# Differential attention on one core: a head's two token tiles taken together, with scores by eight products on all 128 rows

## The chip, the cores and the metric

The kernel runs on one core of a Trainium2 chip. The metric is the device time of one execution in microseconds (us). A core has a matrix engine (TensorE, in the profile PE, with its weight loads as PEld), two engines for element-wise work (VectorE, DVE, and ScalarE, ACT), GpSimd (POOL) and a DMA queue on SyncE (SP). PE multiplies a stationary operand (its weights, at most 128 rows by 128 columns) with a moving one and adds the result into PSUM, a small memory of eight banks of 512 float32 columns. All else lies in SBUF, on 128 partitions ("rows" below). PE executes its instructions strictly in the order of the program text.

## The reference

Two decoder layers on 256 tokens of width 2048, all in float32. Each layer does this, cut to what matters here:

```
h   = RMSNorm(x);  P = h @ W_in          columns [q | k | v | gate_B | gate_C | conv_in], 1024 each
q,k = RMSNorm over 64 numbers            8 heads x 2 maps x 64
s   = q_m k_m^T / 8 + bias, causal       m = 0, 1: two score maps per head
A   = (softmax(s_0) - lam softmax(s_1)) @ v, RMSNorm per head, times a gain
Cv  = gate_B * conv3(gate_C * conv_in)
x   = x + concat([A, Cv]) @ W_out
x   = x + relu(RMSNorm(x) @ W_up)^2 @ W_down
```

A head has 128 columns of q and k, 64 for each map, and 128 of v. The tokens are two tiles of 128. By causality the first tile sees 128 keys, the second 256.

## The kernel before, in words

**Arithmetic.** Every float32 operand is split into a high part (rounded for PE) and a low part (the rest). A product is three products: high x high, high x low, low x high (`TERMS`, line 38). Weights are split as they arrive: `Weights.halves` (line 277) writes `whi` on ScalarE (line 285) and `wlo` on VectorE (line 286).

**Order of PE's work.** The text gives it, and it is manual for PE. In `mixer` (line 602) two halves of four heads each compute q, k and v with `linear` (line 328: a 512-column product for each tile, term and 128 input columns), then follow four gc/ci pairs and four gb products with `linear_t` (line 347: eight products of 512 columns and eight of 256 for each group of weights) and the output projection. Three groups of weights are made ahead (`AHEAD`).

**Ticks.** Small pieces are put between these products. A piece is a Python generator in `Background` (line 55); it yields the number of ticks until it goes on. `linear` ticks after every six products, `linear_t` after every four. So the first half's attention runs among the second half's q, k and v products, and the second half's among the first gc and ci products. `staggered` (line 85) starts the units of an attention some ticks apart.

**q and k.** `qk_norm` (line 458) normalizes a half's q or k, waits 8 ticks, transposes each token tile on PE (line 481) and writes high and low parts with one ScalarE copy (line 484) and one VectorE operation (line 485). Each head's 128 rows hold map 0 in rows 0 to 63 and map 1 in rows 64 to 127.

**Attention.** `attention` (line 489) has a unit for each of 2 tiles x 4 heads, 4 ticks apart, all first tiles ahead of all second tiles:

- scores `sc` (line 503): for each map three products on that map's 64 rows, of 128 or 256 columns;
- bias and row maximum on VectorE (line 506), negation (511), exponentials with their sums on ScalarE (513), reciprocal, c and p on VectorE (516 to 524); 9 ticks after the scores the transposes of p, `ptp` (529), and its split `pT` (531, 532);
- 4 ticks later the products with v, `av` (539): three for each 128 keys, of 128 columns, into one bank for four heads. After the fourth head the bank is copied out (547), squared and normalized (552 to 559), and 9 ticks later transposed (`atp`, 565) and written in parts to `cat` (568, 569), an input of the output projection.

PSUM has three rotating banks for `sc`, `ptp` and the other transposes, one for `av`, and two pairs for the long products. The engines other than PE get their order from the framework's scheduler, and run it in order.

**Setup.** Gains, the bias table and lambda vectors are loaded on POOL's queue at the start (lines 168 to 183) into buffers of their own and used by `small_setup` (line 199) and `load_bias` (line 230).

Of the kernel before, what the change touches and what calls it, by code (L numbers as in the profile page):

```python
# [9 lines left out]
F32 = mybir.dt.float32  # L10
# [91 lines left out]
def trunk(ctx: ExitStack, tc: tile.TileContext, x, w_in, w_out, conv_w, q_norm_g, k_norm_g,  # L102
# [8 lines left out]
    nat = ctx.enter_context(tc.tile_pool(name="nat", bufs=7))  # L111
# [19 lines left out]
    const.tile([P, 40], F32, tag="fill", name="fill")  # L131
# [36 lines left out]
    vec = const.tile([ROWS, P], F32, tag="vec", name="vec")  # L168
    nc.gpsimd.dma_start(vec[0:NCW, :], conv_w.rearrange("l i (k p) -> (l i k) p", p=P))
    for i, g in enumerate((q_norm_g, k_norm_g)):  # L170
        for m in range(2):
            nc.gpsimd.dma_start(
                vec[QG + i * DEPTH:QG + (i + 1) * DEPTH, m * DK:(m + 1) * DK], g)
    nc.gpsimd.dma_start(vec[QG + 2 * DEPTH:MG, :], subln_g)
    nc.gpsimd.dma_start(vec[MG:ROWS, :], mlp_norm_g.rearrange("l (k p) -> (l k) p", p=P))
    lamv = const.tile([1, 4, DEPTH, DK], F32, tag="lamv", name="lamv")
    for i, a in enumerate((lambda_q1, lambda_q2, lambda_k1, lambda_k2)):
        nc.gpsimd.dma_start(lamv[:, i], a[None])
    sel = const.tile([NB + 1, REL], F32, tag="sel", name="sel")
    nc.gpsimd.dma_start(sel, selector)  # L180
    rel = const.tile([NB + 1, 2 * NH], F32, tag="rel", name="rel")
    nc.vector.memset(rel[NB:NB + 1, :], NEG)
    nc.gpsimd.dma_start(rel[0:NB, :], rel_bias)
# [15 lines left out]
    def small_setup():  # L199
# [3 lines left out]
        by_dist = const.tile([2 * NH, REL], F32, tag="bydist", name="by_dist")  # L203
# [12 lines left out]
        prod = const.tile([1, 2, DEPTH, DK], F32, tag="lprod", name="lprod")  # L216
# [13 lines left out]
    def load_bias(l, bpool, bias):  # L230

        if l == 0:
            yield from small_setup()
        revs = []
        for j in range(2):
            rev = bpool.tile([P, NH, S], F32, tag="b", name=f"rev{l}{j}")
            src = by_dist_d[j * NH:(j + 1) * NH, 0:S]
            nc.gpsimd.dma_start(
                rev, bass.AP(src.tensor, src.offset, [[1, P], [REL, NH], [1, S]]))
            revs.append(rev)  # L240
        yield 4
        for h in range(0, NH, 2):
            for j in range(2):
                late(nc.scalar.activation(bias[:, j * NH + h:j * NH + h + 2],
                                          revs[j][:, h:h + 2, ::-1], AF.Copy))
            yield 2
# [141 lines left out]
    class Norm:  # L388
# [31 lines left out]
        def factors(self):  # L420
            while not all(t.ready for t in self.tiles):
                yield 1
            tot = small.tile([P, NT], F32, tag="tot", name="tot")
# [5 lines left out]
            if self.which:  # L429

                self.scale = small.tile([P, 1], F32, tag="rowf2", name="rowf2")
                nc.vector.tensor_mul(self.scale, r[:, 1:2], r[:, 1:2])
                ratio = small.tile([P, 1], F32, tag="ratio", name="ratio")
# [24 lines left out]
    def qk_norm(acc, r, dst, gain, name):  # L458
# [18 lines left out]
        yield 8  # L477
        for t in range(NT):
            tp = bank(f"{name}tp{t}")
            for i in range(4):  # L480
                nc.tensor.transpose(tp[:, i * P:(i + 1) * P], out_[t][:, i * P:(i + 1) * P], ident)
            tp3 = tp.rearrange("p (h c) -> p h c", c=P)
            hi, lo = (dst[:, i, :, t * P:(t + 1) * P] for i in range(2))
            nc.scalar.activation(hi, tp3, AF.Copy, scale=gain)
            nc.vector.scalar_tensor_tensor(lo, tp3, gain, hi.bitcast(F32),
                                           op0=ALU.mult, op1=ALU.subtract)
            yield 1

    def attention(l, qT, kT, v, h0, dst, bias, tmp):

        parts = dst.open()
        avs, r0s = {}, {}

        def unit(t, i):
            W = (t + 1) * P
            h = h0 + i
            s = tmp.tile([P, 2, S], F32, tag="s", name=f"s{h}_{t}")
            mx = small.tile([P, 2], F32, tag="mx", name=f"mx{h}_{t}")
            su = small.tile([P, 2], F32, tag="su", name=f"su{h}_{t}")
            for m in range(2):  # L500
                sc = bank(f"sc{h}_{t}_{m}")
                for n, (a, b) in enumerate(TERMS):
                    nc.tensor.matmul(  # L503
                        sc[:, :W], qT[m * DK:(m + 1) * DK, a, i, t * P:(t + 1) * P],
                        kT[m * DK:(m + 1) * DK, b, i, :W], start=(n == 0), stop=(n == 2))
                nc.vector.tensor_tensor_reduce(
                    out=s[:, m, :W], in0=sc[:, :W], in1=bias[:, 2 * h + m, S - W:],
                    op0=ALU.add, op1=ALU.max, scale=1.0, scalar=-3.0e38,
                    accum_out=mx[:, m:m + 1])
            nm = small.tile([P, 2], F32, tag="nm", name=f"nm{h}_{t}")  # L510
            nc.vector.tensor_scalar_mul(nm, mx, -1.0)
            for m in range(2):
                nc.scalar.activation(s[:, m, :W], s[:, m, :W], AF.Exp, bias=nm[:, m:m + 1],
                                     accum_out=su[:, m:m + 1])
            rc = small.tile([P, 2], F32, tag="rc", name=f"rc{h}_{t}")
            nc.vector.reciprocal(rc, su)
            if i == 0:
                r0s[t] = small.tile([P, 4], F32, tag="r0", name=f"r0_{h0}_{t}")
            nc.vector.tensor_copy(r0s[t][:, i:i + 1], rc[:, 0:1])
            c = small.tile([P, 1], F32, tag="c", name=f"c{h}_{t}")  # L520
            nc.vector.scalar_tensor_tensor(c, su[:, 0:1], rc[:, 1:2], nlam[:, l:l + 1],
                                           op0=ALU.mult, op1=ALU.mult)
            p = tmp.tile([P, S], F32, tag="p", name=f"p{h}_{t}", bufs=2)
            nc.vector.scalar_tensor_tensor(p[:, :W], s[:, 1, :W], c, s[:, 0, :W],
                                           op0=ALU.mult, op1=ALU.add)
            yield 9
            tp = bank(f"ptp{h}_{t}")
            for b in range(t + 1):
                nc.tensor.transpose(tp[:, b * P:(b + 1) * P], p[:, b * P:(b + 1) * P], ident)
            pT = tmp.tile([P, 2, S], F32R, tag="pT", name=f"pT{h}_{t}", bufs=2)  # L530
            nc.scalar.activation(pT[:, 0, :W], tp[:, :W], AF.Copy)
            nc.vector.tensor_sub(pT[:, 1, :W], tp[:, :W], pT[:, 0, :W].bitcast(F32))
            yield 4
            if i == 0:
                avs[t] = ps.tile([P, CH], F32, tag="av", name=f"av{h0}_{t}", bufs=1)
            av = avs[t]
            for k in range(t + 1):
                for n, (a, b) in enumerate(TERMS):
                    nc.tensor.matmul(  # L539
                        av[:, i * P:(i + 1) * P], pT[:, a, k * P:(k + 1) * P],  # L540
                        v[:, b, k, i * P:(i + 1) * P],
                        start=(k == 0 and n == 0), stop=(k == t and n == 2))
            if i < 3:
                return
            r0 = r0s[t]
            ao = wide(f"ao{h0}_{t}")
            nc.scalar.activation(ao, av, AF.Copy)
            ss = small.tile([P, 4], F32, tag="ams", name=f"ams{h0}_{t}")
            junk = wide(f"asq{h0}_{t}")
            for b in range(4):  # L550
                c = slice(b * P, (b + 1) * P)
                nc.scalar.activation(junk[:, c], ao[:, c], AF.Square, accum_out=ss[:, b:b + 1])
            for _ in range(2):
                nc.gpsimd.tensor_tensor(ss, ss, r0, op=ALU.mult)
            f = rstd_of(ss, P, f"a{h0}_{t}", 4)
            f2 = small.tile([P, 4], F32, tag="af2", name=f"af2{h0}_{t}")
            nc.gpsimd.tensor_tensor(f2, f, r0, op=ALU.mult)
            an = wide(f"an{h0}_{t}")
            nc.vector.tensor_tensor(
                an.rearrange("p (g d) -> p g d", d=P), ao.rearrange("p (g d) -> p g d", d=P),  # L560
                f2.unsqueeze(2).to_broadcast([P, 4, P]), op=ALU.mult)
            yield 9
            tp = bank(f"atp{h0}_{t}")
            for b in range(4):
                nc.tensor.transpose(tp[:, b * P:(b + 1) * P], an[:, b * P:(b + 1) * P], ident)
            tp3 = tp.rearrange("p (h c) -> p h c", c=P)
            hi = parts[:, 0, :, t * P:(t + 1) * P]
            nc.scalar.activation(hi, tp3, AF.Copy, scale=s_gain[:, l:l + 1])
            nc.vector.scalar_tensor_tensor(
                parts[:, 1, :, t * P:(t + 1) * P], tp3, s_gain[:, l:l + 1], hi.bitcast(F32),  # L570
                op0=ALU.mult, op1=ALU.subtract)

        yield from staggered([unit(t, i) for t in range(NT) for i in range(4)], 4)
# [28 lines left out]
    def mixer(l, norm, loads):  # L602

        with ExitStack() as scope:
# [4 lines left out]
            weights = Weights(rpool)  # L609
            weights.cut = l == 0  # L610
# [13 lines left out]
            work.start(load_bias(l, bpool, bias), 10)  # L624
# [405 lines left out]
```

## Time and profile before

| what | value |
|---|---|
| median of 3 runs | 2178.3 us (2177.54 to 2178.63) |
| profiled execution, own time | 2181.21 us |
| its span | 2179.4 us |
| score products (line 503) | 192, on 64 rows |
| av products (line 539) | 144, of 128 columns |
| DMA | 446.62 MB, mean 205 GB/s |

The span is the time from the first to the last instruction; the execution's own time holds some 2 us around it. Most views count an engine's busy time. PE's rows overlap, since a product starts before the last one has drained; what a product costs is the distance from its start to the next one's start. "Idle before, releaser" says what ended an engine's wait. The chain of waits follows the work that ended last backwards through whatever released it.

### The profile page before, as it was taken

The page shows a single profiled execution, that of the slowest core. Times are in us where ns is not written, and L with a number is a line of the kernel's source. Part 1 is how long each engine was busy: PE and PEld are TensorE (multiplying, and loading weights), DVE is VectorE, ACT ScalarE, POOL GpSimd, SP SyncE. Part 2 cuts the span into 40 slices and gives each one's busy share as a digit, 9 for nine tenths or more (in the row PEclk, how much of TensorE's full clock was granted, in tenths as well). Part 3 has the DMA queues.
Part 4 walks back from the last instruction along what each step waited for, and adds up shares of the span by engine and source line. Part 5 has one row for each costly group of instructions (what it writes and reads, how often), then busy time and mean ns, then how long its engine had stood idle before and what let it go on. Part 6 is the DMA issues. An engine that isn't in the chain of part 4 may idle for free.

```text
span 2179.4 us, 29050 instructions
## 1 busy us (share of the span) xinstructions
PE 2156.3 (99%) x11066; PEld 1828.2 (84%) x11066; DVE 1604.7 (74%) x2229; ACT 1271.6 (58%) x1718; POOL 136.9 (6%) x194
## 2 busy tenths in 40 slices
PE   8999999999999999999999999999999999999999
PEld 6888888888888888888888888888888888888887
DVE  6677655698888888855566776557988888887554
ACT  6456445566666666644455664446666666665443
POOL 2021100000000000100011111000000000001000
PEclk9999999999999999999999999999999999999999
DMA  7545666476666666577565465656676666666774
GB/s 261 177 154 188 209 184 189 158 242 212 215 217 217 211 213 218 192 265 241 174 212 175 155 210 190 188 166 198 218 219 216 213 213 216 218 209 211 246 241 145
DMA packets 292491, 446.62 MB, mean 205 GB/s; under 512 B 10403, under 2 KB 191221, under 8 KB 292352
## 3 DMA queue, kind: packets, MB, share of 16 engines
q1 hardware_dynamic: 285648, 423.66, 61.4%
q0 software_dynamic: 6656, 21.10, 2.6%
q8 instruction: 86, 1.41, 0.3%
q14 instruction: 53, 0.43, 0.1%
q10 hardware_dynamic: 48, 0.02, 0.0%
HBM read 425.84 MB, written 18.90 MB: 204 GB/s over the span
## 4 chain that ended last, share of the span: by engine, by line
PE 94%; DVE 2%; DMA 2%; ACT 1%; issue 1%; SPq 0%; DVEq 0%; ACTq 0%
PE upc L812 29%; PE dn L972 15%; PE pr L852 13%; PE o L341 8%; PE q L341 4%; PE gc L363 4%; PE ci L363 4%; PE k L341 4%; PE gb L363 4%; PE v L341 4%; PE upw L812 1%; DMA uraw<-in_w_up_dram 1%; PE sc L503 1%; PE av L539 1%; DVE ulo L698 1%
## 5 line engine op out<-in xcount | busy, mean ns | idle before, releaser
L286 DVE TENSOR_TENSOR wlo<-raw,whi 128x1024 fp32r<-128x1024 f32 (+1 forms) x386 | 474.3, 1230 | 383.5 <-ACT whi L285 379.4
L285 ACT ACTIVATE whi<-raw 128x1024 fp32r<-128x1024 f32 (+1 forms) x386 | 406.8, 1055 | 477.6 <-PE dn L972 167.0
L812 PE MATMUL upc<-nT,uhi 128*128 128x512 f32 x1920 | 477.6, 391 | 0.0
L697 ACT ACTIVATE uhi<-uraw 128x1024 fp32r<-128x1024 f32 x256 | 271.0, 1060 | 285.7 <-PE upc L812 254.0
L812 PEld LDWEIGHTS upc<-nT,uhi 128*128 128x128 f32 x1920 | 352.8, 188 | 68.2
L698 DVE TENSOR_TENSOR ulo<-uraw,uhi 128x1024 fp32r<-128x1024 f32 x256 | 312.9, 1222 | 115.5 <-ACT uhi L697 113.1
L972 PE MATMUL dn<-whi,g 128*128 128x512 f32 x1024 | 316.4, 389 | 0.0
L812 PEld LDWEIGHTS upc<-nT,ulo 128*128 128x128 f32 x1920 | 261.9, 190 | 18.7
L812 PE MATMUL upc<-nT,ulo 128*128 128x256 f32 x1920 | 267.7, 282 | 0.0
L972 PEld LDWEIGHTS dn<-whi,g 128*128 128x128 f32 x1024 | 192.2, 188 | 39.7
L972 PE MATMUL dn<-wlo,g 128*128 128x512 f32 x512 | 199.7, 390 | 1.2 <-DVE wlo L286 1.0
L341 PE MATMUL o<-whi,cat 128*128 128x512 f32 x512 | 159.6, 390 | 0.0
L972 PEld LDWEIGHTS dn<-wlo,g 128*128 128x128 f32 x512 | 96.1, 188 | 22.9 <-DVE wlo L286 2.9
L341 PEld LDWEIGHTS o<-whi,cat 128*128 128x128 f32 x512 | 96.1, 188 | 19.8
L341 PE MATMUL o<-wlo,cat 128*128 128x512 f32 x256 | 99.6, 389 | 0.0
L834 POOL DMA_DIRECT2D hid<-h x64 | 35.0, 546 | 950.0 <-ACT h L833 914.1
L852 PE MATMUL pr<-t13h,f 128*128 128x512 f32 x240 | 93.8, 391 | 0.0
L341 PE MATMUL q<-whi,nT 128*128 128x512 f32 x256 | 86.2, 406 | 3.6 <-ACT nT L251 3.6
L341 PE MATMUL k<-whi,nT 128*128 128x512 f32 x256 | 85.3, 399 | 0.0
L852 PE MATMUL pr<-t24h,f 128*128 128x512 f32 x240 | 84.0, 391 | 0.0
L852 PE MATMUL pr<-b2h,f 128*128 128x512 f32 x240 | 84.0, 391 | 0.0
L341 PE MATMUL v<-whi,nT 128*128 128x512 f32 x256 | 83.4, 396 | 0.0
(330 smaller groups left out, 3428.5 us busy)
## 6 DMA issues: line engine op xcount, KB each, us to landing
uraw<-in_w_up_dram SPq DMA_DIRECT2D x128, 1024.0 KB, 5.9
raw<-in_w_in_dram SPq DMA_DIRECT2D x192, 512.0 KB, 3.9
draw<-in_w_down_dram SPq DMA_DIRECT2D x64, 1024.0 KB, 5.0
raw<-in_w_down_dram SPq DMA_DIRECT2D x64, 1024.0 KB, 5.3
raw<-in_w_out_dram SPq DMA_DIRECT2D x64, 512.0 KB, 3.6
hid<-h POOLq DMA_DIRECT2D x64, 256.0 KB, 4.3
back<-hid SPq DMA_DIRECT2D x32, 512.0 KB, 3.3
rev<-by_dist_d POOLq DMA_DIRECT2D x4, 1024.0 KB, 10.1
```

The source lines that it names most:

```text
L285: nc.scalar.activation(hi[:, k], raw[:, k], AF.Copy)
L286: nc.vector.tensor_sub(lo[:, k], raw[:, k], hi[:, k].bitcast(F32))
L341: nc.tensor.matmul(acc[:, t], a.ap[:, pa, k % KG, t * P:(t + 1) * P], (hi, lo)[pw][:, j], start=(k == 0 and n == 0), stop=(k == nk - 1 and ...
L363: nc.tensor.matmul(acc[:, f, 0] if part else acc[:, f], wt[:, k % 4, fs], a.ap[:, 0, k % KG] if part else a.ap[:, :, k % KG], start=(part ...
L503: nc.tensor.matmul(sc[:, :W], qT[m * DK:(m + 1) * DK, a, i, t * P:(t + 1) * P], kT[m * DK:(m + 1) * DK, b, i, :W], start=(n == 0), stop=(n ...
L539: nc.tensor.matmul(av[:, i * P:(i + 1) * P], pT[:, a, k * P:(k + 1) * P], v[:, b, k, i * P:(i + 1) * P], start=(k == 0 and n == 0), stop=( ...
L697: nc.scalar.activation(hi, src, AF.Copy)
L698: nc.vector.tensor_sub(lo, src, hi.bitcast(F32))
L812: nc.tensor.matmul(acc[:, 0] if part else acc, wt[:, k], a.ap[:, 0, k % KG] if part else a.ap[:, :, k % KG], start=(part == 0 and kh == 0 ...
L834: nc.gpsimd.dma_start(hid[i // 2][:, i % 2 * 2 * S:(i % 2 + 1) * 2 * S], u)
L852: nc.tensor.matmul(prods[n], fs[j][:, pa, a], b[pw], start=(j == 0 and m == 0), stop=(stop and m == 2))
L972: nc.tensor.matmul(acc[:, t], f[:, pa, k, t * P:(t + 1) * P], (hi, lo)[pw][:, k % 2], start=(b == 0 and k == 0 and m == 0), stop=(b == NB2 ...
```

## The change

The two tiles of a head become one unit; there are four units a half, 8 ticks apart, with 10 ticks from scores to p's transposes, 4 to the v products and 12 to the output's transposes.

**Scores.** q's high part of a map stands in its own 64 rows of `qT[:, m]`, its low part in the other 64. `kT[:, m]` holds k's high part in both halves, `kL[:, m]` its low part in the map's own half and zeros in the other. A product of 128 rows with `kT` gives two of the three terms, one with `kL` the third. A head takes 2 maps x 2 tiles x 2 = 8 products, four of 128 and four of 256 columns. The split of q and k thus works on half the rows at a time: two ScalarE copies and two VectorE operations a tile for q, four and two for k, and it starts after 12 ticks instead of 8. `kL` is a new buffer, cleared by two POOL operations a layer.

**Softmax.** Both tiles' bias steps, then one negation, four exponentials, one reciprocal, one copy, and c and p for each tile. p's three blocks are transposed as one group and split by one operation on each engine.

**v.** The high part of p meets v's high and low parts in one product of 256 columns; its low part meets v's high part in one of 128. The bank is now one head's; the halves are added by a ScalarE copy (the low halves, into the heads' output `ao`) and a VectorE addition. Squares are taken head by head, the norm once for both tiles.

**Room.** The `wide` buffers go from 7 to 6, some small tiles are made single, a filler grows from 40 to 56 columns, and the setup loads go into one bias buffer of `bpool`, issued in `mixer` instead of ahead of it.

```diff
-    nat = ctx.enter_context(tc.tile_pool(name="nat", bufs=7))
+    nat = ctx.enter_context(tc.tile_pool(name="nat", bufs=6))
...
+    HALF = (slice(0, DK), slice(DK, P))
+    def q_parts(dst):
+        def put(tp3, gain, c):
+            for m, r in enumerate(HALF):
+                hi, lo = dst[r, m, :, c], dst[HALF[1 - m], m, :, c]
+                nc.scalar.activation(hi, tp3[r], AF.Copy, scale=gain[r])
+                nc.vector.scalar_tensor_tensor(lo, tp3[r], gain[r], hi.bitcast(F32),
+                                               op0=ALU.mult, op1=ALU.subtract)
+        return put
+    def k_parts(dst, low):
+        def put(tp3, gain, c):
+            for m, r in enumerate(HALF):
+                hi, lo = dst[r, m, :, c], low[r, m, :, c]
+                nc.scalar.activation(hi, tp3[r], AF.Copy, scale=gain[r])
+                nc.vector.scalar_tensor_tensor(lo, tp3[r], gain[r], hi.bitcast(F32),
+                                               op0=ALU.mult, op1=ALU.subtract)
+                nc.scalar.activation(dst[HALF[1 - m], m, :, c], tp3[r], AF.Copy, scale=gain[r])
+        return put
...
-        yield 8
+        yield 12
...
+        def unit(i):
+            s = tmp.tile([P, 2, 3 * P], F32, tag="s", name=f"s{h}", bufs=2)
+            sc = [bank(f"sc{h}_{m}") for m in range(2)]
+            for flip in range(2):
+                for k in (kT, kL):
+                    for t in range(NT):
+                        W, m = (t + 1) * P, t ^ flip
+                        nc.tensor.matmul(
+                            sc[m][:, OFF[t]:OFF[t] + W], qT[:, m, i, t * P:(t + 1) * P],
+                            k[:, m, i, :W], start=(k is kT), stop=(k is kL))
...
+            yield 10
+            tp = bank(f"ptp{h}")
+            for b in range(3):
                 nc.tensor.transpose(tp[:, b * P:(b + 1) * P], p[:, b * P:(b + 1) * P], ident)
+            pT = tmp.tile([P, 2, 3 * P], F32R, tag="pT", name=f"pT{h}", bufs=1)
+            nc.scalar.activation(pT[:, 0], tp[:, :3 * P], AF.Copy)
+            nc.vector.tensor_sub(pT[:, 1], tp[:, :3 * P], pT[:, 0].bitcast(F32))
             yield 4
+            av = ps.tile([P, CH], F32, tag="av", name=f"av{h}", bufs=1)
+            av = av.rearrange("p (t n c) -> p t n c", t=NT, n=2)
+            for t in range(NT):
+                for k in range(t + 1):
+                    w = slice(OFF[t] + k * P, OFF[t] + (k + 1) * P)
+                    nc.tensor.matmul(av[:, t], pT[:, 0, w], v[:, :, k, i * P:(i + 1) * P],
+                                     start=(k == 0), stop=False, skip_group_check=True)
+                    nc.tensor.matmul(av[:, t, 0], pT[:, 1, w], v[:, 0, k, i * P:(i + 1) * P],
+                                     start=False, stop=(k == t), skip_group_check=True)
+            mine = slice(i * P, (i + 1) * P)
+            nc.scalar.activation(ao[:, :, mine], av[:, :, 1], AF.Copy)
+            nc.vector.tensor_add(ao[:, :, mine], av[:, :, 0], ao[:, :, mine])
...
-        yield from staggered([unit(t, i) for t in range(NT) for i in range(4)], 4)
+        yield from staggered([unit(i) for i in range(4)], 8)
...
+            setup = None
+            if l == 0:
+                setup = setup_loads(bpool.tile([P, 2 * KG * S], F32, tag="b", name="setup"))
...
+            kL = biasp.tile([P, 2, 4, S], F32R, tag="kL", name=f"kL{l}")
+            for m, r in enumerate(HALF):
+                nc.gpsimd.memset(kL[HALF[1 - m], m].bitcast(F32), 0.0)
```

More of the change, by code (lines that the diff above doesn't have):

```diff
@@ L481, in qk_norm @@
                 nc.tensor.transpose(tp[:, i * P:(i + 1) * P], out_[t][:, i * P:(i + 1) * P], ident)
[L482 to L486, printed above, removed]
+            put(tp.rearrange("p (h c) -> p h c", c=P), gain, slice(t * P, (t + 1) * P))
@@ L487, in qk_norm, with attention @@
             yield 1
-    def attention(l, qT, kT, v, h0, dst, bias, tmp):
+    def attention(l, qT, kT, kL, v, h0, dst, bias, tmp):
         parts = dst.open()
-        avs, r0s = {}, {}
-        def unit(t, i):
-            W = (t + 1) * P
-            h = h0 + i
[L497 to L515, printed above, removed]
-            nc.vector.reciprocal(rc, su)
[L517 to L528, printed above, removed]
@@ L557, in unit @@
[L557 to L566, printed above, removed]
@@ new lines, in unit @@
+            yield 12
+            for t in range(NT):
+                tp = bank(f"atp{h0}_{t}")
+                for b in range(4):
+                    nc.tensor.transpose(tp[:, b * P:(b + 1) * P], an_[t][:, b * P:(b + 1) * P],
+                                        ident)
+                tp3 = tp.rearrange("p (h c) -> p h c", c=P)
+                hi = parts[:, 0, :, t * P:(t + 1) * P]
+                nc.scalar.activation(hi, tp3, AF.Copy, scale=s_gain[:, l:l + 1])
+                nc.vector.scalar_tensor_tensor(
+                    parts[:, 1, :, t * P:(t + 1) * P], tp3, s_gain[:, l:l + 1], hi.bitcast(F32),
+                    op0=ALU.mult, op1=ALU.subtract)
+                yield 2
@@ L623, in mixer @@
             bias = biasp.tile([P, 2 * NH, S], F32, tag="bias", name="bias")
[L624 removed]
+            work.start(load_bias(l, bpool, bias, setup), 10)
             hT = norm.tiles
```

137 lines of the change are left out of this document (80 added, 57 removed).

## The prediction

> **What bounds the kernel now.** First the head of the profile's page, with the busy times and the shares of the chain that ended last.
>
> ```profile
> span 2179.4 us, 29050 instructions
> PE 2156.3 (99%) x11066; PEld 1828.2 (84%) x11066; DVE 1604.7 (74%) x2229; ACT 1271.6 (58%) x1718; POOL 136.9 (6%) x194
> ...
> PE 94%; DVE 2%; DMA 2%; ACT 1%; issue 1%; SPq 0%; DVEq 0%; ACTq 0%
> ```
>
> PE is busy for 99% of the span and is 94% of the chain. What shortens PE's stream shortens the kernel, as long as PE does not begin to wait. So I need the stream price of the products that go and that come, and the slack of the engines which feed PE. The second view is the chain of waits as a list in order of time: start, length, piece, count. Around the first half's heads (second tile from 109.04 on) it shows
>
> ```profile
> 102.43 4.12 PE q L341 x18
> 106.55 0.49 PE sc L503 x6
> ...
> 109.04 4.13 PE k L341 x18
> 113.17 0.56 PE sc L503 x6
> ...
> 115.33 0.28 PE av L539 x3
> 115.62 0.13 PE ptp L529
> 115.75 4.13 PE k L341 x18
> ```
>
> and in the second half's heads, between the gc and ci products,
>
> ```profile
> 172.63 0.49 PE sc L503 x6
> ...
> 173.79 0.11 PE ptp L529
> ...
> 176.22 0.49 PE sc L503 x6
> ...
> 184.09 0.56 PE sc L503 x6
> ...
> 185.32 0.29 PE av L539 x3
> 185.61 0.13 PE ptp L529
> ...
> 188.04 0.56 PE sc L503 x6
> ...
> 201.18 0.62 PE av L539 x6
> ```
>
> For the undisturbed pace of a product I take the timeline of an up-projection stretch (start, length, group):
>
> ```profile
> 661.83 1.77 PE L812 MATMUL upc<-nT,uhi 128*128 128x512 f32 x7
> 663.44 1.11 PE L812 MATMUL upc<-nT,ulo 128*128 128x256 f32 x8
> 664.39 0.40 PE L852 MATMUL pr<-t13h,f 128*128 128x512 f32 x1
> ```
>
> Seven 512-column products start within 1.61 us, 0.23 each; eight of 256 columns within 0.95, 0.12 each, every one with its own weights. Six av products of 128 columns take 0.62, and a p transpose of 128 columns 0.11 to 0.13; I take 0.11 for 128 columns. Half the columns cost nearly as much.
>
> **The products that go and come.** A score unit costs more than its own row, since the products beside it are slowed. So I take whole rounds and subtract the rest. First half: the 24 k or q products of a round at 0.229 make 5.50. The first tile's round (102.43 to 109.04) is 6.61; less 5.50 and 0.41 for av and ptp (the same as in the next round) leaves 0.70. The second tile's (109.04 to 115.75) is 6.71, which leaves 0.80. Second half: a round of four ticks holds 8 products of 512 and 8 of 256 columns, 2.79. The first tile's round (172.63 to 176.22) is 3.59; less 2.79 and 0.11 leaves 0.69. The second's (184.09 to 188.04) is 3.95; less 2.79 and 0.42 leaves 0.74. A head therefore pays 1.50 or 1.43 for its twelve 64-row products, 1.47 on average.
>
> New are eight 128-row products, four of 128 and four of 256 columns: 4 x 0.11 + 4 x 0.12 = 0.92. Saved: 0.55 a head, for 16 heads **8.8 us**.
>
> For v a head has had 3 + 6 products, 0.29 + 0.62 = 0.91. It will have three of 256 and three of 128 columns, 3 x 0.12 + 3 x 0.11 = 0.69. Saved: 0.22 x 16 = **3.5 us**. The three transposes of p stay, in one group instead of two, as do those of q, k and the output: nothing. PE's stream thus loses **12.3 us**.
>
> That the switch to 64 rows is what slows the neighbours is seen in the timeline at one unit:
>
> ```profile
> 99.87 0.39 PE L341 MATMUL q<-whi,nT 128*128 128x512 f32 x1
> 100.18 0.56 PE L503 MATMUL sc<-kT,qT 64*128 64x128 f32 x6
> 100.67 0.50 PE L341 MATMUL q<-whi,nT 128*128 128x512 f32 x1
> 101.01 0.40 PE L341 MATMUL q<-wlo,nT 128*128 128x512 f32 x1
> ```
>
> The last q product before it holds PE for 0.31 instead of 0.23 and the first one behind it for 0.34; the six themselves run in 0.49, less than six steps of 0.11, so the two maps' products do run side by side. The Trainium skill, TensorEngine Tiling (Array Packing), section Overview, promises up to twice the speed for a contraction of 64 rows or fewer, as two row tiles work in parallel; that speaks against this change. By that rule alone six products cost three steps and the sum gains nothing from the scores (third rival). Its section Tiling Modes also says that a change of mode drains TensorE. The trace bears out both: six in 0.49, and 0.19 lost at the neighbours.
>
> **What this asks of ScalarE and VectorE.** The groups by line for 165 to 202 us (count, busy us, mean ns) and two windows (PE, PEld, DVE, ACT, POOL busy) give the prices.
>
> ```profile
> L286 DVE TENSOR_TENSOR wlo<-raw,whi 128x1024 fp32r<-128x1024 f32 x11 | 13.4, 1222 | 0.9 <-ACT whi L285 0.7
> L506 DVE CUSTOM_DVE_ANT_0 s<-sc,bias 128x256 f32<-128x256 f32 x8 | 3.3, 419 | 1.4 <-PE sc L503 1.4
> L521 DVE SCALAR_TENSOR_TENSOR c<-su,rc,nlam 128x1 f32<-128x1 f32 x8 | 2.7, 336 | 0.0
> L506 DVE CUSTOM_DVE_ANT_0 s<-sc,bias 128x128 f32<-128x128 f32 x8 | 2.1, 287 | 1.5 <-PE sc L503 1.5
> L524 DVE SCALAR_TENSOR_TENSOR p<-s,c 128x256 f32<-128x256 f32 x4 | 1.9, 482 | 0.0
> L285 ACT ACTIVATE whi<-raw 128x1024 fp32r<-128x1024 f32 x10 | 10.5, 1055 | 3.1 <-ACT pT L531 1.7 <-PE gc L363 0.8 <-ACT s L513 0.6
> L513 ACT ACTIVATE s<-s,nm 128x256 f32<-128x256 f32 x8 | 4.0, 503 | 2.3 <-DVE nm L511 2.3
> L513 ACT ACTIVATE s<-s,nm 128x128 f32<-128x128 f32 x8 | 3.1, 394 | 1.1 <-DVE nm L511 1.1
> ...
> 150.00:165.00 15.00, 15.00 (x78) 12.64 (x77) 8.34 (x10) 9.03 (x19) 2.55 (x5) 1.00 0.52 164
> 165.00:202.00 37.00, 37.00 (x250) 31.91 (x249) 31.57 (x102) 25.03 (x65) 3.15 (x6) 1.00 0.45 148
> ```
>
> Scores to p is now one chain for both tiles: four bias steps 2 x 0.42 + 2 x 0.29 = 1.41, four exponentials 2 x 0.50 + 2 x 0.39 = 1.79, two c 0.67, two p about 0.83 (0.48, and 0.35 estimated for the shorter tile), and some 0.65 for the negation, accumulator read, reciprocal and copy, a rough estimate at half a c each: **5.4 us** unqueued, against 3.3 for the second tile alone. What queueing adds is read at the last unit of before (timeline):
>
> ```profile
> 192.05 0.63 PE L503 MATMUL sc<-kT,qT 64*128 64x256 f32 x6
> 198.84 0.48 DVE L524 SCALAR_TENSOR_TENSOR p<-s,c 128x256 f32<-128x256 f32 x1
> 201.64 0.41 PE L529 MATMUL ptp<-ident,p 128*128 128x128 f32 x2
> ```
>
> From 192.68 to 199.32 are 6.6 us, so 3.3 of queueing, and 2.3 of slack. New: 5.4 + 3.3 = 8.7. The cover is ten ticks: 2.5 weight groups x 2.79 = 7.0, plus the neighbour heads' p transposes 0.36, v products 0.69 and scores 0.92, together 9.0. In the first half ten ticks are 60 products, 13.7 us, and nothing is late. In the second 0.3 us is left, and less for the first head, which has no head before it (7.9). VectorE's work there hardly falls (one negation, reciprocal and copy less a head, an add more), while the stretch falls by about 4 x 0.75 = 3 us: 31.6 of 34, 93% instead of 85%. Queued behind these steps stands wlo on VectorE and whi on ScalarE, for which PE waits three groups later. I take **0.2 us** a head as the mean wait here, 1.6 in 8 heads; the bounds are 0 and 2.0 (first rival). From p's transposes to v the cover is four ticks, 2.8 plus their own 0.36; before, pT took 1.7 (no queue) to 3.2 (behind a wlo) of as much, and its two longer pieces add about 0.25: 0.1 a head, **0.8** in 8 heads.
>
> The split of q and k works on half the rows at a time. No row has a 64-row copy here, but one has 16 rows:
>
> ```profile
> L204 DVE COPY by_dist<-rps x1: 544/544/544, 26.7 to 26.7; 16x383 f32<-16x383 f32 x1
> L484 ACT ACTIVATE kT<-k01tp,gains x2: 688/688/689, 150.9 to 152.7; 128x512 fp32r<-128x512 f32 x2
> ```
>
> Cost goes with columns, not rows. A half costs between 0.34 and 0.69; I take 0.69. k's copies on ScalarE go from 1 to 4 a tile, 3 x 2 x 0.69 = 4.1 us more, in the 15 us before the second half's scores: 9.0 + 4.1 = 13.2 of 15. q's (+1 on each engine a tile) have a whole product more to land. k's copies move from tick 8 to 12; from there to the first score are 8.0 us of products plus 0.9 of transposes. ScalarE's eight copies and three whi are 8.7, the evictions of v 1.3 more. So the first score is late by 0 to 2; I take 0.5 a layer, **1.0 us**. In the first half the cover is 10.4: nothing.
>
> Hidden altogether: the small loads moved into a bias buffer are the same issues in the same order at the head of POOL's queue, and pass no other issue on it or on SP's (if they came too late for the first bias product: one for one, PE being in order). Clearing kL is POOL work, and POOL is 94% free. Two score banks held at once leave the third for p's transposes, whose turn comes two ticks later. Six wide buffers for seven, and the buffers made single, sit behind PE. Shifted addresses may move the waits at the stage changes by a microsecond either way.
>
> **Sum:** -12.3 + 1.6 + 0.8 + 1.0 = **-8.9 us**. The profiled execution (2181.2, of which 2179.4 span) would be 2172.3. The median of the runs shown is 2178.3, so the forecast is **2169.4**.
>
> **Rivals.** *The chain outruns its cover* (slower). Place: p's transposes of the second half's heads, where PE waits in order. It decides once scores to p takes over 10.3 us, where 8 heads x 1.3 and the other waits, 1.8, eat the 12.3. With one more wlo and one more whi ahead of it than seen (2.3), 5.4 + 5.6 = 11.0 against 9.0, each head waits 2.0: -12.3 + 16 + 1.8 = +5.5, **2183.8**. For it: VectorE at 93%; against it: a slack of 2.3 where the queue was longest. Chance 0.12.
>
> *The edge cost stays*: something that the scores keep, their wait on a bank say, makes the edges, not the row switch. Three side-by-side steps are 0.33 to 0.36, so some 0.4 a unit is edge; one a head left is 16 x 0.4 = 6.4: -8.9 + 6.4 = -2.5, **2175.8**. Against it: av and ptp come with waits too and show no such edge. 0.07.
>
> *Pairing was worth its rows*: if three steps, 0.35, were a unit's whole price, the scores would go from 0.70 to 0.92 a head, +3.5, and cancel v's gain: the waits are left, +3.4, **2181.7**. This is the rule of the Trainium skill's tiling page taken alone. The rounds of 6.61 and 3.95 speak against it: 0.03.
>
> *VectorE becomes the pace* in the second half: its heads, half of the 12.3, save nothing; with the waits less the 2.5 that belong to those heads: -6.2 + 1.0 + 2 (wlo late at the end of the stretch) = -3.2, **2175.1**. 0.10.
>
> *All is hidden*: -12.3, **2166.0**, within the forecast's own range.
>
> **Chances and range.** Forecast, 2164 to 2173.5: 0.68; the three rivals near no change: 0.20; slower: 0.12. A measurement of this kernel can tell about 0.2%, 4.4 us, from no change: faster 0.68, within 0.20, slower 0.12. The range, 2164.0 to 2181.0, leaves out the slower rival, most of the pairing and a little below.
>
> **What would show it.** Right: eight score products of 128 rows in about 0.9 us with the product before and behind them at 0.23; six av products in 0.7; PE idle before p's transposes in the second half for under 2 us in all. Wrong: PE waiting for p by more than 1.3 a head, for whi or wlo among gc and ci, or for kT or kL at the first score; or edges of 0.3 still around the scores.

## The result and the profile after

The median of nine runs is 2171.55 us (2170.46 to 2174.78), against 2178.42 us for nine runs of the kernel before beside them (2177.54 to 2179.4). The ratio is 0.9967 (95%: 0.9958 to 0.9976): 0.33% faster, 6.9 us. The forecast was 2169.4, its range 2164 to 2181.

The profiled execution of after took 2170.46, its span is 2168.7. That is 1.1 below its median, and before's profiled execution stood 2.8 above its own, so of the 10.7 us between the spans only 6.9 are in the medians. First the head of the page of after.

```profile
span 2168.7 us, 28831 instructions
PE 2144.8 (99%) x10954; PEld 1825.8 (84%) x10954; DVE 1611.0 (74%) x2197; ACT 1293.5 (60%) x1742; POOL 133.3 (6%) x178
...
PE 95%; DVE 2%; DMA 1%; ACT 1%; issue 1%; SPq 0%; DVEq 0%; ACTq 0%
```

PE still sets the time, with 112 products less. Next the chain of waits of after (start, length, piece, count), in the first half's heads and then in the second's.

```profile
99.16 0.92 PE sc L539 x8
100.08 2.75 PE q L350 x12
102.83 0.33 PE ptp L570 x3
103.16 4.12 PE q L350 x18
...
108.64 0.12 PE av L581
...
108.81 0.17 PE av L581
...
109.04 0.18 PE av L581
...
109.28 2.82 PE k L350 x12
...
162.96 1.49 PE sc L539 x7
164.45 2.53 PE gc L372 x8
...
167.42 1.41 PE gc L372 x8
...
179.60 0.93 PE sc L539 x8
```

Eight score products cost 0.92 and 0.93, and the products around them run at 0.23 each (2.75 for twelve). The six v products take 0.64 from the first one's start to that of the k product behind them (108.64 to 109.28), and the twelve products behind them 2.82 instead of 2.75, so a head pays 0.71. One row of this list is not like the others: the first scores of the second half, at 162.96, took 1.49 for seven products, and the eight gc products behind them 2.53 instead of 1.41.

To compare the kernels I took every group of short products that stands inside PE's long streams and counted what it adds there: the distance between the long products around it, less their own pace. All these groups together take 73.25 us in before and 66.12 in after, 7.1 less. In the second half's first score group 2.9 us (layer 0) and 2.24 (layer 1) are more than its 0.92, and 0.19 more is found once in the first half: 5.3 together. Without these, the stream is shorter by 7.1 + 5.3 = **12.4 us**. So the stream lost what the forecast said, and one wait took much of it back. The list of PE's waits in after has it (us in total, times, longest).

```profile
PE sc L539 <- ACT kT L490: 4.0, 2, 2.0
```

There is no row for p's transposes and none for the v products. Why kT is late is seen in ScalarE's timeline of after (start, length, group, idle before and its releaser).

```profile
153.24 0.67 ACT L487 ACTIVATE kT<-k01tp,gains 64x512 fp32r<-64x512 f32 x1
154.49 0.68 ACT L487 ACTIVATE kT<-k01tp,gains 64x512 fp32r<-64x512 f32 x1 [0.58 <-PE k01tp L516]
155.94 1.06 ACT L294 ACTIVATE whi<-raw 128x1024 fp32r<-128x1024 f32 x1 [0.76 <-PE v L350]
...
159.85 1.06 ACT L294 ACTIVATE whi<-raw 128x1024 fp32r<-128x1024 f32 x1
160.93 0.69 ACT L695 ACTIVATE v<-v,rowf 128x512 fp32r<-128x512 f32 x1
161.65 1.26 ACT L490 ACTIVATE kT<-k01tp,gains 64x512 fp32r<-64x512 f32 x2
```

Eight half-row copies at about 0.69, two whi and one v eviction are 8.3 us of work; the engine stood idle for 0.58 and 0.76 in front of instructions whose turn it was, and the last of k's copies ends at 162.91, 9.7 after the first one began. PE reads it in its second score product, whose turn was at 160.94: the rows of map 1, 256 columns, so both tiles' copies. ScalarE was not full in this stage (columns: stretch; its length; busy PE, PEld, DVE, ACT, POOL with counts; granted clock, the share of its full clock that PE was given; DMA share; GB/s):

```profile
150.00:165.00 15.00, 12.98 (x66) 11.05 (x65) 10.52 (x18) 11.46 (x15) 2.21 (x4) 0.95 0.52 167
165.00:199.00 34.00, 34.00 (x212) 30.19 (x212) 28.42 (x81) 23.83 (x66) 1.29 (x1) 0.97 0.52 167
...
160.00:163.41 3.41, 1.39 (x11) 1.19 (x9) 2.59 (x3) 3.33 (x5) 0.00 (x0) 1.00 0.41 137
163.41:166.82 3.41, 3.41 (x14) 2.92 (x14) 2.62 (x10) 1.27 (x2) 0.00 (x0) 0.50 0.44 148
1235.18:1238.59 3.41, 2.27 (x13) 1.85 (x11) 2.43 (x3) 3.32 (x5) 0.00 (x0) 1.00 0.50 154
1238.59:1242.01 3.42, 2.53 (x17) 2.29 (x18) 2.43 (x11) 2.58 (x4) 0.00 (x0) 1.00 0.50 158
```

ScalarE was busy for 11.46 of 15. The last four rows, two around each layer's wait, show a second loss: behind layer 0's wait the granted clock is 0.50 for 3.4 us, and the products run slower there: 1.49 - 0.91 = 0.58 for the seven scores (0.91 is what the same seven took in layer 1, 1239.48 to 1240.39), and 2.53 - 1.41 = 1.12 for the eight gc products. Behind layer 1's wait of the same length the clock stayed at 1.00. So the wait cost 2.0 twice, and a slower clock another 1.7 once.

### The profile page after: what moved, and what is told of

Its sections match the earlier page's. It is cut to its first block, busy times and chain, and to the rows that moved or that the text cites. A ratio compares the mean times of both kernels' runs of the same rounds, so it can differ in the third digit from the quotient of the medians.

```text
span 2168.7 us, 28831 instructions
## 1 busy us (share of the span) xinstructions
PE 2144.8 (99%) x10954; PEld 1825.8 (84%) x10954; DVE 1611.0 (74%) x2197; ACT 1293.5 (60%) x1742; POOL 133.3 (6%) x178
## 3 DMA queue, kind: packets, MB, share of 16 engines
q8 instruction: 86, 1.41, 0.3%
## 4 chain that ended last, share of the span: by engine, by line
PE 95%; DVE 2%; DMA 1%; ACT 1%; issue 1%; SPq 0%; DVEq 0%; ACTq 0%
PE upc L867 30%; PE dn L1027 16%; PE pr L907 13%; PE o L350 8%; PE q L350 4%; PE ci L372 4%; PE gb L372 4%; PE k L350 4%; PE gc L372 4%; PE v L350 4%; PE upw L867 1%; PE sc L539 1%; DMA back<-hid 1%; PE tpn L414 1%; DMA uraw<-in_w_up_dram 0%
## 6 DMA issues: line engine op xcount, KB each, us to landing
rev<-by_dist_d POOLq DMA_DIRECT2D x4, 1024.0 KB, 10.7
```

## The experiments

Two questions had to be settled. Where do the 12.4 us come from: from the merging of two groups of 64-row products into one, from the full rows, or from the wider v products? And why is the first score late: because k's split starts too late, or because of what stands ahead of it in ScalarE's order? A third was whether p's chain really had cover. Each experiment's text names its theories with letters of its own. Times are medians; ratios are to before on the same chip.

**Scores on 64 rows again, but in one group:**

```diff
-            for flip in range(2):
-                for k in (kT, kL):
-                    for t in range(NT):
-                        W, m = (t + 1) * P, t ^ flip
+            for t in range(NT):
+                for m in range(2):
+                    W, r = (t + 1) * P, HALF[m]
+                    for n, k in enumerate((kT, kL, kL)):
                         nc.tensor.matmul(
-                            sc[m][:, OFF[t]:OFF[t] + W], qT[:, m, i, t * P:(t + 1) * P],
-                            k[:, m, i, :W], start=(k is kT), stop=(k is kL))
+                            sc[m][:, OFF[t]:OFF[t] + W], qT[r, m, i, t * P:(t + 1) * P],
+                            k[r, m, i, :W], start=(n == 0), stop=(n == 2))
```

> The changed kernel, whose scores go back to products on 64 rows: six for each tile and the two tiles in one group, twelve a head. The third product repeats the second one's operands in place of low x high, so that it stays on the same rows. Everything else, the half-row copies of q and k too, stays. A: the old price was three side-by-side steps plus one edge of about 0.4 us for each group, made by the switch to 64 rows. Then a head's scores cost 0.33 + 0.36 + 0.4 = 1.1 us against 0.93 of the changed kernel: 16 x 0.17 = 2.7 us slower than it. B: the price belongs to each tile's six products and is not an edge. Then a head pays 1.47 again, 8.6 us slower. C: the row switch costs nothing, and the old edges came from something that the merged unit lacks. Then a head pays 0.7, 3.7 us faster.

It took 2170.48 (ratio 0.9963, 0.9949 to 0.9976), by which nothing seems lost. The chain of waits shows the group, and the list of PE's waits and its timeline the rest.

```profile
110.18 2.82 PE k L350 x12
113.00 0.89 PE sc L539 x12
113.90 2.96 PE k L350 x12
```

```profile
PE sc L539 <- ACT kT L490: 2.0, 2, 1.0
```

```profile
162.91 1.26 ACT L490 ACTIVATE kT<-k01tp,gains 64x512 fp32r<-64x512 f32 x2
...
163.65 0.39 PE L539 MATMUL sc<-kT,qT 64*128 64x128 f32 x2 [1.02 <-ACT kT L490]
```

The twelve run in 0.89, and the twelve k products behind take 2.96, where twelve behind full-row scores take 2.75: with these 0.21 the group costs 1.10 in the first half and 1.08 in the second, 0.17 more than eight products on full rows. Over 16 heads that is 2.7 us. One group instead of two is thus 1.47 - 1.10 = 0.37 of the gain a head, full rows the other 0.17.

The 2.7 are hidden in the median by a shorter wait, 1.0 instead of 2.0 a layer, without a slow clock behind it. These scores do not read the second copies of k (line 490) at all: each map stays on its own rows. Yet PE goes on at 163.65, as the last copy but one ends. The first product that reads map 1 of both tiles starts at 164.04, while the last copy still runs (to 164.17). By the kernel's text, what the last copy but one releases is the bank of the first tile's transposes of k, one of the three that the scores share. So in after the first score waits for two things that end with these copies: the data until the last, a bank until the last but one.

**v's wide product split in two:**

```diff
-                    nc.tensor.matmul(av[:, t], pT[:, 0, w], v[:, :, k, i * P:(i + 1) * P],
-                                     start=(k == 0), stop=False, skip_group_check=True)
+                    for b in range(2):
+                        nc.tensor.matmul(av[:, t, b], pT[:, 0, w], v[:, b, k, i * P:(i + 1) * P],
+                                         start=(k == 0 and b == 0), stop=False,
+                                         skip_group_check=True)
```

> The changed kernel, whose v products of 256 columns are each split into two of 128 with the same weights; the same result. A: a product of 128 columns costs PE 0.11 us because its weights are loaded each time, so a head's v products go from 0.70 to 9 x 0.11 = 0.99: 16 x 0.28 = 4.5 us slower than the changed kernel. B: columns alone count, or the second product with the same weights is cheap: 0 to 1 us slower.

It took 2173.9 (0.9981, 0.9971 to 0.9990). The chain:

```profile
109.17 0.22 PE av L582 x2
109.39 0.12 PE av L585
109.51 0.22 PE av L582 x2
```

Two halves and the narrow product behind them take 0.34 (109.17 to 109.51), where one wide and one narrow product take 0.23 in after (108.81 to 109.04): each of the three splits costs 0.11. A head pays 1.01 to 1.03 instead of 0.71, +0.31, 5.0 us in 16 heads. The medians differ by 2.4 only, the profiled spans by 4.8. The first score is 2.0 late in both layers of both kernels, but the clock falls behind it in the profiled execution of after alone. The split is made again below without that wait.

**Before, with its score products on all 128 rows** (six each, as they were):

```diff
-                        sc[:, :W], qT[m * DK:(m + 1) * DK, a, i, t * P:(t + 1) * P],
-                        kT[m * DK:(m + 1) * DK, b, i, :W], start=(n == 0), stop=(n == 2))
+                        sc[:, :W], qT[:, a, i, t * P:(t + 1) * P],
+                        kT[:, b, i, :W], start=(n == 0), stop=(n == 2))
```

> The kernel before, whose six score products of a tile run on all 128 rows instead of 64 (both maps' rows are summed into each score, so the scores are other numbers); counts, columns, units and waits are unchanged. A: the edges come from the switch to 64 rows: no edge is left, six products in series cost 0.67 (128 columns) and 0.73 (256), a head 1.40 against 1.47: about 1 us faster than before. B: the edges come from what the scores wait for: six in series and an edge of 0.4 each, 2.2 a head: 11 us slower.

It took 2177.42 (0.9999, 0.9990 to 1.0008). First the timeline around a unit, to be read beside the prediction's at 99.87, then the chain.

```profile
100.30 0.39 PE L341 MATMUL q<-whi,nT 128*128 128x512 f32 x1
100.53 0.78 PE L503 MATMUL sc<-kT,qT 128*128 128x128 f32 x6
101.15 0.44 PE L341 MATMUL q<-whi,nT 128*128 128x512 f32 x1
```

```profile
106.98 0.62 PE sc L503 x6
107.61 1.44 PE q L341 x6
```

On full rows the product ahead of the unit holds PE for 0.23 (100.30 to 100.53) and the one behind for 0.28 (to 101.43); on half rows it was 0.31 and 0.34: the loss at the edges comes, for the most part, with the switch of rows. But the six no longer run side by side, 0.62 instead of 0.49, and a unit costs 0.69 to 0.73 instead of 0.70 to 0.80. The two effects cancel for a group of six: pairing wins in the steps what the switch loses at the edges.

**k's split four ticks earlier**, all else as after:

```diff
-    def qk_norm(acc, r, put, gain, name):
+    def qk_norm(acc, r, put, gain, name, ticks=12):
...
-        yield 12
+        yield ticks
...
-                work.start(qk_norm(acc, r, k_parts(kT, kL), k_gain[:, l:l + 1], f"k{l}{half}"))
+                work.start(qk_norm(acc, r, k_parts(kT, kL), k_gain[:, l:l + 1], f"k{l}{half}", 8))
```

> The changed kernel with k's transposes and copies 8 ticks after its products, as before, instead of 12. q's stay at 12. A: PE waits at the second half's first score because ScalarE's eight copies of k start too late for it. Started four ticks (5.5 us) earlier they are done in time: the wait of 2.0 us in each layer goes, and with what is queued behind it some 4 to 5 us, so 2167. B: ScalarE is full there, and the copies end when they end: the wait stays above 1.5 a layer, no change. C: the earlier transposes themselves wait for the second normalized tile of k on VectorE: a wait of 1 to 2 us moves to k's transposes, no change.

It took 2164.84 (0.9937, 0.9924 to 0.9949), its five runs lying within 0.33 us. The second half's start in its chain, and the end of k's copies in ScalarE's timeline:

```profile
161.09 0.93 PE sc L539 x8
162.02 1.40 PE gc L372 x8
```

```profile
156.28 0.69 ACT L490 ACTIVATE kT<-k01tp,gains 64x512 fp32r<-64x512 f32 x1
156.99 1.06 ACT L294 ACTIVATE whi<-raw 128x1024 fp32r<-128x1024 f32 x1
```

The last copy ends at 156.97, four us ahead of the scores; PE waits nowhere there, and the gc products behind run at full pace. The groups between the long products fall from 66.12 to 61.15. With the 1.1 of the slowed gc products that makes 6.1, against 5.6 between the spans and 6.7 between the medians. So the late k, with the clock that fell behind it, was the whole of what after had lost.

**The attention three ticks later** (k's split at tick 12 as in after):

```diff
-                work.start(attention(l, qT, kT, kL, v, h0, cat[half], bias, tmp), 3)
+                work.start(attention(l, qT, kT, kL, v, h0, cat[half], bias, tmp), 6)
```

> The changed kernel with attention started 6 ticks after v instead of 3; k's copies stay at tick 12. A: the wait at the second half's first score is only a matter of that tick: three ticks more are 2.1 us of gc products, so of the 2.2 to 2.9 us of wait a layer some 0.5 is left, and the kernel gains 4 to 5 us, 2167. B: ScalarE's queue as a whole is late there, and the scores' own chain then comes into the same crowd: the wait moves from the first score to p's transposes, no gain.

It took 2169.36 (0.9959, 0.9947 to 0.9972). PE's waits:

```profile
PE sc L539 <- DVE qT L477: 2.8, 2, 1.4
...
PE sc L539 <- ACT kT L490: 0.8, 2, 0.4
```

The wait for kT falls to 0.4 a layer. A new one of 1.4 a layer comes for the first half's last head. Its scores now stand right behind the transposes of the second half's q and wait for VectorE's work on them; they read the first half's q, so by the kernel's text it is the shared bank again. The experiment shows two waits at once and tells the two theories of the late k apart only in part.

**k's second copy on VectorE:**

```diff
-                nc.scalar.activation(dst[HALF[1 - m], m, :, c], tp3[r], AF.Copy, scale=gain[r])
+                nc.vector.tensor_scalar_mul(dst[HALF[1 - m], m, :, c], tp3[r], gain[r])
```

> The changed kernel with the second copy of k's high part (four of the eight ScalarE copies of each k) made on VectorE; ticks unchanged. A: ScalarE's order is the cause, where the last two copies stand behind a whi and an eviction of v that themselves wait for PE: four copies fewer, and the last one is done about 1.5 us ahead of the score; the wait of 2.2 to 2.9 us a layer goes, 4 to 5 us gained. B: k's transposes at tick 12 are too late for any engine: VectorE, with 0.75 us a copy and wlo of 1.22 between, ends as late, and PE waits for it instead, by 1 us or more.

It took 2167.62 (0.9953, 0.9941 to 0.9966). PE's waits, then VectorE's timeline:

```profile
PE sc L539 <- DVE kT L490: 2.9, 2, 1.4
```

```profile
158.80 1.23 DVE L295 TENSOR_TENSOR wlo<-raw,whi 128x1024 fp32r<-128x1024 f32 x1
...
161.60 0.76 DVE L488 SCALAR_TENSOR_TENSOR kL<-k01tp,gains,kT 64x512 fp32r<-64x512 f32 x1
162.38 0.76 DVE L490 TENSOR_SCALAR kT<-k01tp,gains 64x512 fp32r<-64x512 f32 x1
```

From the first copy (154.14 in this execution) to the end of the last it takes 9.0 instead of 9.7, and PE's turn comes 7.7 after the first one, as in after. So four copies less on ScalarE bring 0.6 a layer (and no slow clock follows); the last copies now stand behind a wlo on VectorE as they stood behind a whi on ScalarE. Moving the load to the other engine thus cures little: at tick 12 the split comes too late for either.

**k at tick 8, and p's transposes 8 ticks behind the scores instead of 10:**

```diff
-            yield 10
+            yield 8
```

> The changed kernel with k's copies at tick 8 (2164.8) and, besides, 8 ticks instead of 10 from scores to p's transposes. Its slack there was 0.98, 0.25, 1.07 and 0.43 us for the four heads of a second half. A: two ticks are 1.4 us of cover, and the chain of VectorE and ScalarE is as long as before: waits of 0.4, 1.15, 0.3 and 1.0, 2.9 a layer, 5.7 in all: 2170.5. B: the chain is paced by PE, whose waits give VectorE time: the second and later heads regain it, 1 to 2.5 in all: 2166 to 2167. C: ten ticks were more than needed, no change.

It took 2170.86 (0.9967, 0.9954 to 0.9979), 6.0 above the same kernel with 10 ticks. PE's waits:

```profile
PE ptp L570 <- DVE s L565: 3.7, 8, 0.7
```

The eight heads among the gc and ci products now wait for p, 3.7 us of idle. The groups between the long products grow by 6.9 against 10 ticks; what the rest of that is was not resolved. In after, the same chain from scores to p ends 0.98, 0.25, 1.07 and 0.43 us before PE's turn in the four heads. The cover is there, but not by two ticks.

**k at tick 8, with the 64-row scores in one group**, the edits of the first and the fourth experiment together:

> The changed kernel with k's copies at tick 8 and scores by twelve products on 64 rows in one group (the third product repeats the second one's operands in place of low x high). A: with no wait for kT left the price of the form shows in the time: a head's scores 1.10 instead of 0.93: 2.6 us slower than 2164.8, so 2167.4. B: the form makes no difference in time, as between the changed kernel and its own 64-row version.

It took 2168.62 (0.9951, 0.9937 to 0.9965). A group costs 1.08 to 1.11, as before. With no wait to hide in, the loss is seen: 3.8 us against the fourth experiment by the medians, where 16 x 0.17 makes 2.7. The runs of this one spread from 2166.7 to 2169.6, so the 1.1 between is not resolved.

**k at tick 8, v's wide product split**, the second and the fourth together:

> The changed kernel with k's copies at tick 8 and each v product of 256 columns split into two of 128; the same result. A: with no wait for kT the PE price shows whole: 1.02 a head instead of 0.71, 16 x 0.31 = 5.0 us slower than the same kernel with the 256-column products, measured beside it: 2169.8 if that is 2164.8. B: as between the changed kernel and its own split version, only 2 to 3 us.

It took 2170.39 (0.9959, 0.9947 to 0.9972), 6.4 above the twin below on the same chip, for a group cost of 1.01 to 1.03 against 0.71, which makes 5.0; the 1.4 between is not explained. The term is real, and it was partly hidden in the second experiment.

**k at tick 10:**

> The changed kernel with k's copies at tick 10. A: each tick of v's products is 1.4 us, two ticks are 2.7, and the wait at tick 12 was 2.2 to 2.9 us a layer: at tick 10 it is 0 to 0.3, and the time is that of tick 8 within 0.6 us. B: the order that ScalarE is given decides and not the tick: the last copies stand behind v's eviction again, and 1 us or more a layer stays.

It took 2165.27 (0.9936, 0.9923 to 0.9948). Its chain has no late score either:

```profile
161.29 0.93 PE sc L539 x8
162.22 1.40 PE gc L372 x8
```

Two ticks are enough, so the split was late by little. It was expected within 0.6 us of tick 8 and came 1.3 above its twin below; the runs of the two overlap (2164.6 to 2166.2 against 2163.1 to 2164.8), and the profiled spans differ by 0.2.

**k at tick 8 again**, beside the last two:

> The kernel with k's copies at tick 8 once more, beside the two others on one chip: 2164.8 again within 1.5 us; above 2167 the earlier figure was luck of its chip.

It took 2164.01 (0.9929, 0.9915 to 0.9943), 14.8 below before on that chip (2178.8). This version is better than both kernels: 0.63 to 0.71% below before in its two tries, where the change as made gave 0.33%.

## Why the prediction was right, and where it was off

**PE's stream: right.** The forecast was -12.3; the groups gave -12.4. New scores: 0.92 forecast, 0.92 to 0.94 measured. New v products: 0.69 forecast, 0.71 measured. The reason given was right too: the edges come with the switch of rows, as before on full rows shows: nothing lost ahead of the unit, 0.05 behind it. The prediction's estimate of some 0.4 of edge a unit agrees with the merged group: six steps of 0.11 to 0.12 and 0.4 make 1.1, measured 1.10. An old head was two such edges and about 0.7 of steps, a new one 0.92 of steps and no edge.

**p's chain: forecast 1.6, measured 0.** The sum of 8.7 for scores to p was good (7.6 to 8.7 in the four heads of layer 1, from the start of the product behind the scores) and so was the cover of 9.0 (8.0 to 9.0). Two parts of the sum were off and cancelled, which was luck: the two p took 0.74 and 0.34 instead of 0.83 together, the two c 0.21 each instead of 0.34. The first head's cover was 8.8 and not 7.9, since the first half's output transposes stand in it. Put against each other they left 0.3, and the prediction added a mean wait of 0.2 for the spread of the queue; the spread stayed within the slack in this order. The cover of 8 ticks shows how near it is.

**pT to v: forecast 0.8, measured 0.** No wait of v's products for pT stands in PE's list.

**The first score: the term that was mis-sized.** The prediction said "So the first score is late by 0 to 2; I take 0.5 a layer, 1.0 us". PE waiting for kT at the first score is also one of the signs that the prediction named for being wrong, and it came, though its three signs of being right came too. The wait is 2.0 in each layer, the score groups' excess 5.3 in all, and with the slowed gc products 6.4. Its own figures spoke for more than 0.5: 8.7 and 1.3 of ScalarE work against a cover of 8.9. What was left out is idle time. The cover of 8.9 runs from k's first transposes (152.03) to PE's turn (160.94); 1.2 of it had passed, behind these transposes and one of the three whi, when the first copy began (153.24), and 7.7 were left. And the work behind that was taken as one block, while in order the engine stood idle for 1.34: 8.3 + 1.34 = 9.7, less 7.7 is the 2.0. The price of a half-row copy, 0.69, was right (0.66 to 0.69 for 64 x 512), so its upper bound was the true value. That ScalarE would be busy for 13.2 of 15 us was too much (11.46), and load was not what decided.

**The slower clock behind the wait** was in no term: 1.7 in the profiled execution of after, and by the granted clocks of its other runs (last section) not there alone.

**The sum.** -12.4 + 0 + 0 + 6.4 = -6.0, measured by medians -6.9, forecast -8.9: the first score took 5.4 more than forecast, the other waits 2.4 less. What the profiled spans show beyond this, another 4.7, lies outside the changed groups (0.6 at the start, 1.1 and 1.8 in the MLP stages, the rest in small pieces); 3.9 of it is the two executions' distance from their medians. That the total came within 2.0 us of the forecast is thus in part luck: two errors in the waits, of 5.4 and 2.4, stand against each other.

**The rivals.** The chain that outruns its cover didn't happen; its place was right, as the waits at 8 ticks show. No edge stayed. Pairing was not worth its rows, though it is worth some 0.2 a head in the steps: 0.92 against 1.10 - 0.4. VectorE did not become the pace: 28.42 of 34, 84%, where 93% was forecast.

## What to carry to other kernels

A split into half-row pieces multiplies the instructions of an in-order engine at full price; when it also starts later, lay its pieces out on the timeline of the engine, with what stands between them, from the moment its input is there to the moment PE wants the last one, and add the idle in front of each. Before half-row products are judged by their own speed, weigh what the switch costs at both ends of a group: here six products were no faster paired than on all rows. And when a change saves what its steps promise and the time does not show it, look for a single late hand-over: two ticks here were worth 6.3 us, nearly as much as the 6.9 of the change itself.

## What the runs showed of the hardware

The granted clock fell to 0.50 from 163.41 to 166.82 us in after, behind a PE wait of 2.0 us. The same wait in layer 1 left it at 1.00, and so did two waits of 2.0 at these places with v's products split and the shorter ones of other experiments (1.0 and 1.4). What decided is where the wait fell. In each kept trace all changes of the clock lie whole steps of 3.413 us apart: in after, 166.82 is one step behind 163.41, and 2167.03, at the kernel's end, is 586 steps behind 166.82. The four rows at the end of the result are stretches of this grid. Layer 0's wait lies whole in one of them, where PE was busy for 1.39 of 3.41, and the next one ran at half clock. Layer 1's wait is cut by an edge at 1238.59, and PE was busy for 2.27 and 2.53 in the two parts. With v's products split an edge cuts both waits, and no stretch has less than 1.83 busy. From the first full clock on, every whole stretch of the thirteen kept traces with 2.02 us of idle PE or more was followed by half clock, and none with 1.94 or less was. An estimate from these numbers: a wait of 2.02 fits whole into a stretch of 3.41 from 1.39 of 3.41 starting points, so about four in ten of such waits are punished, by chance.

The Trainium skill, TensorE: Matmul & The Clock Gate, section Part 1: The HAM clock gate, says that the rate halves after an idle window of about 3.4 us whose grid runs freely. The half rate, the length and the grid agree with the trace; the stretch that counted as idle here was not empty, as PE was busy for 1.39 of it.

The mean granted clock of each run fits this. It is 0.998 or 0.999 in all nine runs of after. Of the ten with v's products split, the four at 1.000 took 2172.4 to 2173.7 us, the five at 0.999 2173.2 to 2176.4, and the one at 0.998 2177.2. All ten runs with k at tick 8 alone, where the wait is gone, show 1.000. So the clock is part of the spread of after's runs (4.3 us, against 0.3 and 1.7 in the two tries with k at tick 8); how much of it was not shown.

A copy of 64 rows and 512 columns took 0.67 to 0.69 on ScalarE, as much as one of 128 rows (0.69 before). On VectorE it took 0.74 to 0.76. A product of 256 columns cost 0.12, and two of 128 columns 0.22: half the columns saved almost nothing.
